# Small constants fetched behind the third step, a shorter lead for small transfers, and a shorter row of steps at the last tile's end, in a planned hybrid-decoder kernel

## The chip, the cores and the metric

The kernel runs on one core of one Trainium2 chip. The metric is the device time of one launch in microseconds (us), the median of several runs. Engines are named as the profile names them: PE (TensorE matmuls), DVE (VectorE), ACT (ScalarE), POOL (GpSimd) and SP (SyncE), which issues every DMA of this kernel.

## The reference

One layer of a hybrid decoder over a prompt of 2048 tokens and 8 single sample tokens, all in float32. The in-projection has 1024 rows and 4104 columns: eight groups of 512 columns, and 8 gate columns.

```python
h = rmsnorm(x, norm_w)
p = einsum('btd,de->bte', h, w_in)
hq, hf, hi, hz, gq, gk, gv, gz, gb, ga = split(p)
fg = lb + (1 - lb) * sigmoid(hf)               # lb from hg_lb_logits
o_hg, s_hg = hgrn2(hq, 1 - fg, hi, log(fg))    # 4 heads: S = diag(f) S + k v^T
qkv = silu(causal_conv4([gq | gk | gv], conv_w))
o_gdn, s_gdn = gated_delta(l2norm(q), l2norm(k), v, sigmoid(gb), g(ga))   # 4 heads
o = [rmsnorm(o_hg) * silu(hz) | rmsnorm(o_gdn) * silu(gz)]
y = rmsnorm(x + o @ w_out, final_norm)
```

The prompt runs through chunked forms of both recurrences; the samples take one recurrent step from given states. Outputs are both `y`, and the new states of prompt and samples.

## The kernel before, in words

**Arithmetic.** A float32 product is made of three PE passes over rounded parts: `xh`·`wh`, `xl`·`wh`, `xh`·`wl`, where the high part comes from a rounding copy and the low part is what that copy lost. For a piece of the in-projection's weights, DMA brings `raw` (256 KB), ACT writes `wh` and POOL writes `wl`. For tokens, PE transposes `xt` into `ps_x`, ACT writes `xh` and DVE `xl`. The out-projection has the same shape with `wor`, `woh`, `wol`, `oh` and `ol`.

**Order of the work.** `build` walks over a list of steps (loop at L1528): two halves of the prompt, four heads in each, and for each head the eight column groups, 512 tokens at a time. A step starts generators (projection, what follows it, the chains of the two recurrences); they record instructions through a wrapper, so that all instructions outside of PE bear line L404. Nothing is issued in the order of the program: `Model.plan` (L114) plays the recorded instructions forward and back on a model of the five queues (`play`, L155), eight passes, and fixes the best order found on every engine. For SP's DMAs it knows three things: the earliest moment of an issue, which is `AHEAD` = 30 us ahead of the instruction's due time (L173, L229); at most `LANES` = 8 transfers under way (L221); and one wire with a price by size and by the length of the contiguous run (L384).

**Constants.** Six small loads bring the convolution weights, the bound logits, the two head norms (all four into one tile `rows`, L1386 to L1390) and two gate vectors (`ald`). `small_ones` (L1402) then transposes `rows` on PE (`ps_rows`) and works out the constants that the heads' steps read; its last result is an integer `low`, which SP reads into a register.

**A gated-delta head.** For each head in each half of the prompt (eight times in all), a matrix is solved by blocks: DVE works `ti` out in 62 small steps (`xa`, `tm`, `ti`), four DMAs store it (`td<-ti`), four bring it back in another layout (`ut<-td`), DVE transposes it (`tn`), and PE goes on with `ps_v` and `ps_u`. The eight samples have a chain of their own beside it: `bcs<-dl` (4 KB, out), `db<-bcs` (the same spread over 128 partitions, 512 KB), eight scalings of `db` on ACT, `gate_s` and `a_bc` for the decay, and eight updates `S<-S,a_bc,db` on DVE.

**The end.** `out_proj` multiplies token tiles of 128 by `w_out`, adds the residual by halves of 512 columns (`xt<-ps_y,xt` on DVE), takes the sum of squares of each half on ACT (`jk`, `fss`), and `finish` (L1631) makes the reciprocal root on POOL (`frs`), scales by it and by `final_norm`, and stores. The last tile is scaled and stored in two halves.

## Time and profile before

| | us |
|---|---|
| median of 3 runs | 1253.29 |
| lowest, highest | 1249.16, 1253.98 |
| the profiled execution | 1249.11 |
| its span, first to last instruction | 1247.3 |
| PE busy | 1209.9 |
| DVE, ACT, POOL busy | 901.7, 516.8, 302.8 |

The profiled execution took 1249.11 us, of which 1247.3 are its span and 1.8 lie around it. It is as fast as the fastest of the three runs and 4.18 below their median. The mean granted clock of TensorE was 0.992 of full speed.

### The profile page before, as it was taken

To read this page: it belongs to the slowest core of one execution; us is meant where nothing else is said; L and a number is where in the kernel's file an instruction comes from. 1 tells how busy PE (TensorE), PEld (TensorE's weight loads), DVE (VectorE), ACT (ScalarE), POOL (GpSimd) and SP (SyncE) were. 2 spreads that over 40 slices of the span, in tenths; PEclk is the share of its full clock that TensorE was granted. 3 is DMA by queue.
4 is the path that set the end of the run, shared out by engine and by line. 5 is a ranking of instruction groups with operands and counts; after the bars stand their busy time and mean duration, and the time that the engine had idled before them with its cause. 6 is when DMAs were issued, how large, how long until landed. Compare 5 with 4: busy or idle time off the path is not lost.

```text
span 1247.3 us, 21811 instructions
## 1 busy us (share of the span) xinstructions
PE 1209.9 (97%) x8003; PEld 1045.9 (84%) x8003; DVE 901.7 (72%) x2301; ACT 516.8 (41%) x1517; POOL 302.8 (24%) x292
## 2 busy tenths in 40 slices
PE   7999999999899999989999999999999999999996
PEld 6988998989798889987787888887888887877885
DVE  5467986879687887889687868795787687854433
ACT  5436423633374326552464226323622464223221
POOL 5222221322133323312233214321322130000000
PEclk8999999999999999999999999999999999999998
DMA  6122443232433421333233332222233227442452
GB/s 198 40 59 60 63 60 87 63 73 57 128 86 73 105 74 35 106 120 77 59 93 70 41 77 47 58 52 61 68 71 77 56 68 222 150 130 88 142 161 91
DMA packets 143541, 107.51 MB, mean 86 GB/s; under 512 B 25611, under 2 KB 126281, under 8 KB 143417
## 3 DMA queue, kind: packets, MB, share of 16 engines
q1 hardware_dynamic: 143424, 106.02, 33.2%
q8 instruction: 65, 1.06, 0.3%
q14 instruction: 52, 0.42, 0.1%
HBM read 82.23 MB, written 23.91 MB: 85 GB/s over the span
## 4 chain that ended last, share of the span: by engine, by line
PE 81%; DMA 8%; DVE 6%; ACT 1%; SPq 1%; issue 1%; POOL 1%; POOLq 0%; DVEq 0%; ACTq 0%
PE ps_pj L517 47%; PE ps_y L517 14%; PE po_g L517 2%; PE po_h L517 2%; PE ps_kq L517 2%; PE ps_u L517 2%; DMA xt<-in_x_prompt_dram 1%; SPq L404 1%; DMA wor<-in_w_out_dram 1%; PE ps_s L517 1%; PE ps_g L517 1%; DMA raw<-in_w_in_dram 1%; PE ps_hu L517 1%; PE ps_ks L517 1%; PE ps_o L524 1%
## 5 line engine op out<-in xcount | busy, mean ns | idle before, releaser
L517 PE MATMUL ps_pj<-xh,wh 128*128 128x512 f32 (+2 forms) x1328 | 468.6, 353 | 7.4 <-ACT pre L404 2.9
L517 PE MATMUL ps_pj<-xl,wh 128*128 128x512 f32 (+2 forms) x1328 | 464.7, 350 | 0.4 <-DVE xl L404 0.4
L517 PE MATMUL ps_pj<-xh,wl 128*128 128x512 f32 (+2 forms) x1328 | 463.9, 350 | 0.7 <-POOL wl L404 0.6
L517 PEld LDWEIGHTS ps_pj<-xh,wh 128*128 128x128 f32 x1328 | 252.3, 190 | 33.3 <-ACT pre L404 3.3
L517 PEld LDWEIGHTS ps_pj<-xh,wl 128*128 128x128 f32 x1328 | 251.8, 190 | 26.0 <-POOL wl L404 1.1
L517 PEld LDWEIGHTS ps_pj<-xl,wh 128*128 128x128 f32 x1328 | 252.2, 190 | 24.4 <-DVE xl L404 0.6
L404 POOL TENSOR_TENSOR wl<-raw,wh 128x512 fp32r<-128x512 f32 x128 | 170.0, 1331 | 368.9 <-ACT wh L404 302.2
L404 ACT ACTIVATE wh<-raw 128x512 fp32r<-128x512 f32 x128 | 80.4, 630 | 162.5 <-PE ps_pj L517 115.8
L517 PE MATMUL ps_y<-woh,oh 128*128 128x512 f32 x256 | 101.0, 396 | 2.1 <-ACT woh L404 2.1
L517 PE MATMUL ps_y<-wol,oh 128*128 128x512 f32 x256 | 100.7, 394 | 0.3 <-DVE wol L404 0.3
L517 PE MATMUL ps_y<-woh,ol 128*128 128x512 f32 x256 | 100.2, 394 | 0.0
L404 DVE TENSOR_TENSOR tm<-xa,ti 128x248 f32<-128x248 f32 (+30 forms) x248 | 85.3, 344 | 16.9 <-DMA xa<-ad 9.0
L404 DVE TENSOR_TENSOR ti<-ti,tm 128x248 f32<-128x248 f32 (+30 forms) x248 | 90.7, 366 | 7.5
L404 ACT ACTIVATE jk<-xt 128x512 bf16<-128x512 f32 (+2 forms) x54 | 39.9, 740 | 117.3 <-DVE xt L404 79.1
L404 POOL TENSOR_TENSOR rso<-sso,mhalf 128x4 f32<-128x4 f32 x32 | 34.8, 1087 | 154.5 <-DVE sso L404 140.1
L517 PEld LDWEIGHTS ps_y<-woh,oh 128*128 128x128 f32 x256 | 48.1, 188 | 11.9 <-ACT woh L404 2.5
L517 PEld LDWEIGHTS ps_y<-wol,oh 128*128 128x128 f32 x256 | 48.2, 188 | 10.2 <-DVE wol L404 0.8
L517 PEld LDWEIGHTS ps_y<-woh,ol 128*128 128x128 f32 x256 | 48.1, 188 | 9.9 <-DVE ol L404 0.5
L404 POOL TENSOR_TENSOR frs<-fss,mhalf 128x1 f32<-128x1 f32 (+1 forms) x17 | 9.4, 555 | 191.5 <-DVE fss L404 191.5
L404 DVE TENSOR_TENSOR xt<-ps_y,xt 128x512 f32<-128x512 f32 (+1 forms) x34 | 23.5, 690 | 44.5 <-PE ps_y L517 44.2
L404 ACT ACTIVATE s_hg<-s_hg,e 128x128 f32<-128x128 f32 x80 | 31.8, 398 | 46.3 <-DVE s_hg L404 41.7
L404 ACT ACTIVATE uu<-ps_u,gam 128x128 f32<-128x128 f32 x64 | 23.4, 365 | 59.7 <-PE ps_u L517 59.3
(291 smaller groups left out, 2124.3 us busy)
## 6 DMA issues: line engine op xcount, KB each, us to landing
raw<-in_w_in_dram SPq DMA_DIRECT2D x128, 256.0 KB
xt<-in_x_prompt_dram SPq DMA_DIRECT2D x30, 512.0 KB
og_d<-sz SPq DMA_DIRECT2D x32, 256.0 KB
og<-og_d SPq DMA_DIRECT2D x32, 256.0 KB
out_dram<-xt SPq DMA_DIRECT2D x15, 512.0 KB
gb<-gate_r SPq DMA_DIRECT2D x16, 256.0 KB
xa<-ad SPq DMA_DIRECT2D x32, 128.0 KB
out_dram<-S SPq DMA_DIRECT2D x8, 512.0 KB
```

The costliest lines, as they stand in the source:

```text
L404: r = fn(*args, **kw)
L517: r = T.matmul(out, lhsT=lhsT, rhs=rhs, start=start, stop=stop)
L524: r = T.transpose(out, in_, idn)
```

## The change

Three things are done. The six small loads move into `small_ones`, and that generator starts at the fourth step (`i == 3`) and not ahead of the loop. In the planner, a transfer whose price on the wire is at most 0.5 us may be issued 15 us ahead of its due time and no more, others 30 as before, and in the first 16 us a transfer of short runs (under 2048 bytes) is priced 1.7 times as high. At the last tile, the first half's sum of squares gets its division and its epsilon early, and the first half its factor `final_norm`; at the end the second half is multiplied by `final_norm` on DVE, one instruction joins the two sums, and after the root ACT scales the first half and DVE the second.

```diff
-                    ready[i] = max(0.0, rank[i] - AHEAD)
+                    ready[i] = max(0.0, rank[i] - self.ahead(i))
...
             if k == "S":
+                if t < 16.0 and sort:
+                    late *= 1.7
                 wire = max(t + 0.8, wire)
...
-                    ready[j] = max(ready[j], rank[j] - AHEAD)
+                    ready[j] = max(ready[j], rank[j] - self.ahead(j))
...
+    def ahead(self, i):
+
+        return AHEAD if self.recs[i][2][1] > 0.5 else AHEAD / 2
...
-            return 0.4, size * 4e-3 / (330.0 if r >= 2048 else 130.0 if r >= 512 else 60.0 if r >= 128 else 6.5), False
+            return 0.4, size * 4e-3 / (330.0 if r >= 2048 else 130.0 if r >= 512 else 60.0 if r >= 128 else 6.5), r < 2048
...
-        rows = tmp.tile([64, P], F32, tag="tmp", name="rows")
-        Q.dma_start(rows[0:48], conv_w[0].rearrange("j (c p) -> (j c) p", p=P))
-        Q.dma_start(rows[48:56], hg_lb_logits.rearrange("l (c p) -> (l c) p", p=P))
-        Q.dma_start(rows[56:57], hg_out_norm)
-        Q.dma_start(rows[57:58], gdn_out_norm)
         wait(lambda: {0, 1} <= xs[0][2])
...
         def small_ones():
+            rows = tmp.tile([64, P], F32, tag="tmp", name="rows")
+            Q.dma_start(rows[0:48], conv_w[0].rearrange("j (c p) -> (j c) p", p=P))
+            Q.dma_start(rows[48:56], hg_lb_logits.rearrange("l (c p) -> (l c) p", p=P))
+            Q.dma_start(rows[56:57], hg_out_norm)
+            Q.dma_start(rows[57:58], gdn_out_norm)
+            Q.dma_start(ald[:, 0:4], gdn_a_log[0].partition_broadcast(P))
+            Q.dma_start(ald[:, 4:8], gdn_dt_bias[0].partition_broadcast(P))
             yield from ready(rows[0:58], slot=MID)
...
-        Q.dma_start(ald[:, 0:4], gdn_a_log[0].partition_broadcast(P))
-        Q.dma_start(ald[:, 4:8], gdn_dt_bias[0].partition_broadcast(P))
         consts = small_ones()
-        start(consts)
...
+            if i == 3:
+                start(consts)
             if i == 6:
...
                 def finish(y, n, ss, dst, pieces):
-                    V.tensor_tensor(ss[:n, 0:1], ss[:n, 0:1], ss[:n, 1:2], op=ALU.add)
-                    V.tensor_scalar(ss[:n, 0:1], ss[:n, 0:1], 1.0 / D, EPS, op0=ALU.mult, op1=ALU.add)
+                    if pieces > 1:
+                        V.tensor_tensor(y[:n, 512:], y[:n, 512:], fnb[:n, 512:], op=ALU.mult)
+                        V.scalar_tensor_tensor(ss[:n, 0:1], in0=ss[:n, 1:2], scalar=1.0 / D, in1=ss[:n, 0:1], op0=ALU.mult, op1=ALU.add)
+                    else:
+                        V.tensor_tensor(ss[:n, 0:1], ss[:n, 0:1], ss[:n, 1:2], op=ALU.add)
+                        V.tensor_scalar(ss[:n, 0:1], ss[:n, 0:1], 1.0 / D, EPS, op0=ALU.mult, op1=ALU.add)
...
+                    if pieces > 1:
+                        A.activation(y[:n, 0:512], y[:n, 0:512], AF.Copy, scale=rs[:n])
+                        V.tensor_scalar(y[:n, 512:], y[:n, 512:], rs[:n], None, op0=ALU.mult)
+                        Q.dma_start(dst[:, 512:], y[:n, 512:])
+                        Q.dma_start(dst[:, 0:512], y[:n, 0:512])
...
+                        if hf == 0 and i + 1 == len(order):
+                            V.tensor_scalar(ss[:n, 0:1], ss[:n, 0:1], 1.0 / D, EPS, op0=ALU.mult, op1=ALU.add)
+                            V.tensor_tensor(y[:n, 0:512], y[:n, 0:512], fnb[:n, 0:512], op=ALU.mult)
```

What the planner makes of it shows in the order of the queues. The first place is SP at the start of the program. Before (`rows` are the constants, `raw` the weights, `xt` the tokens, `csr` a convolution state):

```order
L404 DMA xt<-in_x_prompt_dram 128x512 x3
L404 DMA rows<-in_conv_w_dram 48x128
L404 DMA rows<-in_gdn_out_norm_dram 1x128
L404 DMA rows<-in_hg_lb_logits_dram 8x128
L404 DMA rows<-in_hg_out_norm_dram 1x128
L404 DMA xt<-in_x_prompt_dram 128x512
L404 DMA xt<-in_x_prompt_dram 128x1024
L404 DMA raw<-in_w_in_dram 128x4x128
```

With the change, the same queue from the fourth piece of `raw` on:

```order
L410 DMA raw<-in_w_in_dram 128x4x128
L410 DMA xt<-in_x_sample_dram 8x512
L410 DMA xt<-in_x_prompt_dram 128x1024
L410 DMA xt<-in_x_sample_dram 8x512
L410 DMA raw<-in_w_in_dram 128x4x128 x2
L410 DMA rows<-in_conv_w_dram 48x128
L410 DMA rows<-in_hg_lb_logits_dram 8x128
L410 DMA rows<-in_hg_out_norm_dram 1x128
L410 DMA rows<-in_gdn_out_norm_dram 1x128
L410 DMA csr<-in_state_gdn_conv_dram 24x512 x3
```

The constants stood ahead of the third piece of the weights; they now stand behind the sixth, and `ps_rows` has moved on PE behind 78 projecting matmuls and 44 transposes, where it had none and 16 ahead of it.

The second place is SP at the second half of the second solve, some 300 us into the run. Before:

```order
L404 DMA out_dram<-S 128x8x128
L404 DMA bcs<-dl 8x128
L404 DMA db<-bcs 128x1024
L404 DMA gate_s<-a_s 8x4
L404 DMA a_bc<-gate_s 128x32
L404 DMA td<-ti 32x256 x4
L404 DMA gb<-gate_r 128x512
L404 DMA raw<-in_w_in_dram 128x4x128
L404 DMA og_d<-sz 128x512
L404 DMA ut<-td 32x8x32 x4
L404 DMA gb<-gate_r 128x512
```

With the change:

```order
L410 DMA out_dram<-S 128x8x128
L410 DMA gb<-gate_r 128x512
L410 DMA td<-ti 32x256 x4
L410 DMA ut<-td 32x8x32 x4
L410 DMA og_d<-sz 128x512
L410 DMA gb<-gate_r 128x512
L410 DMA raw<-in_w_in_dram 128x4x128
L410 DMA bcs<-dl 8x128
L410 DMA og_d<-sz 128x512
L410 DMA db<-bcs 128x1024
L410 DMA gate_s<-a_s 8x4
L410 DMA raw<-in_w_in_dram 128x4x128
```

The two trips of the solve (`td`, `ut`) stood behind the samples' four transfers; now they stand ahead of them, and `a_bc` follows behind the last row shown.

The third place is DVE at the program's end: the additions of the last tile's two halves, and what follows. Before:

```order
L404 TENSOR_TENSOR xt_19868<-ps_y,xt_19868 128x512 x2
L404 TENSOR_TENSOR fss<-fss 128x1
L404 TENSOR_SCALAR fss<-fss 128x1
L404 SCALAR_TENSOR_TENSOR xt_19868<-xt_19868,frs,nwb 128x512 x2
L1820 UNCONDITIONAL_BRANCH x2
```

With the change:

```order
L410 TENSOR_TENSOR xt_19870<-ps_y,xt_19870 128x512
L410 TENSOR_SCALAR fss<-fss 128x1
L410 TENSOR_TENSOR xt_19870<-xt_19870,nwb 128x512
L410 TENSOR_TENSOR xt_19870<-ps_y,xt_19870 128x512
L410 TENSOR_TENSOR xt_19870<-xt_19870,nwb 128x512
L410 SCALAR_TENSOR_TENSOR fss<-fss 128x1
L410 TENSOR_SCALAR xt_19870<-xt_19870,frs 128x512
```

The second multiplication by `nwb` (which holds `final_norm`) stands ahead of the instruction that joins the two sums.

## Rows read from the trace of the kernel before

**Rows 1.** The page: busy time of the engines.
```profile
PE 1209.9 (97%) x8003; PEld 1045.9 (84%) x8003; DVE 901.7 (72%) x2301; ACT 516.8 (41%) x1517; POOL 302.8 (24%) x292
```

**Rows 2.** Waits of PE over the whole span: us in total, times, longest.
```profile
PE ps_rows L524 <- DMA rows<-in_conv_w_dram: 4.8, 1, 4.8
PE ps_v L517 <- DVE tn L404: 3.9, 2, 3.3
```

**Rows 3.** Timeline of SP, opening: start us, us, instruction, count.
```profile
6.91 2.68 SPq L404 DMA_DIRECT2D rows<-in_conv_w_dram  x1
...
13.58 0.22 SPq L404 DMA_DIRECT2D rows<-in_hg_out_norm_dram  x1
...
25.80 3.43 SPq L404 DMA_DIRECT2D raw<-in_w_in_dram  x2
```

**Rows 4.** Timeline of PE, opening; in brackets idle time and its releaser.
```profile
17.00 0.33 PE L524 MATMUL ps_rows<-ident,rows 58*128 58x58 f32 x1 [4.82 <-DMA rows<-in_conv_w_dram]
...
28.87 0.39 PE L517 MATMUL ps_pj<-xh,wl 128*128 128x256 f32 x1 [0.59 <-POOL wl L404]
```

**Rows 5.** The chain that ended last, opening: start us, us, what.
```profile
17.23 9.58 DMA raw<-in_w_in_dram
```

**Rows 6.** Two stretches by engine: busy us, instructions; PEclk; DMA share, GB/s.
```profile
30.00:40.00 10.00, 10.00 (x88) 9.87 (x86) 9.03 (x16) 6.66 (x18) 3.04 (x3) 1.00 0.17 44
...
325.00:330.00 5.00, 4.04 (x51) 3.58 (x54) 3.51 (x15) 0.00 (x0) 0.00 (x0) 0.66 0.19 44
```

**Rows 7.** Timeline of SP, 300 to 322 us.
```profile
301.40 1.90 SPq L404 DMA_DIRECT2D bcs<-dl  x1
311.54 0.34 SPq L404 DMA_DIRECT2D db<-bcs  x1
...
314.76 0.33 SPq L404 DMA_DIRECT2D a_bc<-gate_s  x1
315.14 1.82 SPq L404 DMA_DIRECT2D td<-ti  x4
...
317.52 0.40 SPq L404 DMA_DIRECT2D raw<-in_w_in_dram  x1
...
318.64 2.00 SPq L404 DMA_DIRECT2D ut<-td  x4
...
321.44 0.34 SPq L404 DMA_DIRECT2D og_d<-sz  x1
```

**Rows 8.** Timeline of DVE, 311 to 334 us.
```profile
311.52 0.17 DVE L404 TENSOR_TENSOR ti<-ti,tm 128x8 f32<-128x8 f32 x1
...
325.19 0.71 DVE L404 STREAM_TRANSPOSE tn<-ut 128x512 f32<-128x512 f32 x1 [3.63 <-DMA ut<-td]
...
333.35 0.86 DVE L404 COPY v<-ps_v 64x256 f32<-64x256 f32 x2
```

**Rows 9.** Timeline of ACT, first scaling of the samples' `db`.
```profile
315.23 0.40 ACT L404 ACTIVATE db<-db,smp 128x128 f32<-128x128 f32 x1 [5.20 <-DMA db<-bcs]
```

**Rows 10.** Timeline of SP and DVE, the first head's trip of the solve.
```profile
178.11 1.72 SPq L404 DMA_DIRECT2D td<-ti  x4
...
184.62 0.71 DVE L404 STREAM_TRANSPOSE tn<-ut 128x512 f32<-128x512 f32 x1 [0.60 <-DMA ut<-td]
```

**Rows 11.** Timeline of PE and DVE where the out-projection begins, and the last solve.
```profile
1050.36 0.72 PE L517 MATMUL ps_y<-woh,oh 128*128 128x512 f32 x2 [2.11 <-ACT woh L404]
...
1092.13 0.71 DVE L404 STREAM_TRANSPOSE tn<-ut 128x512 f32<-128x512 f32 x1
...
1113.39 0.69 PE L517 MATMUL ps_v<-tn,la 128*64 128x64 f32 x16
```

**Rows 12.** Timeline of DVE, the program's end.
```profile
1237.46 0.69 DVE L404 TENSOR_TENSOR xt<-ps_y,xt 128x512 f32<-128x512 f32 x1 [4.75 <-PE ps_y L517]
...
1238.94 0.16 DVE L404 TENSOR_TENSOR fss<-fss 128x1 f32<-128x1 f32 x1 [0.79 <-ACT jk L404]
...
1240.01 1.41 DVE L404 SCALAR_TENSOR_TENSOR xt<-xt,frs,nwb 128x512 f32<-128x512 f32 x2 [0.73 <-POOL frs L404]
```

More of the change, by code (lines that the diff above doesn't have):

```diff
@@ L1636, in finish @@
                     yield
+                    if pieces > 1:
[3 more added lines that the diff above has]
+                        Q.dma_start(dst[:, 0:512], y[:n, 0:512])
+                        alive[0] -= 1
+                        return
                     w = D // pieces
```

## Prediction

> **What bounds the kernel now.** I read the page first. PE is busy for 1209.9 of 1247.3 us, 97% [rows 1], and no other engine for more than 72%. So only 37 us are open to a change of order: stretches in which PE stands, and the stretches at half clock that follow some of them. The second view is PE's own waits, to see what they are made of: the longest is 4.8 us for `rows` at the opening, the next 3.3 us for `tn`, a step of the second head's solve [rows 2]. The third is the clock by stretch: from 325 to 330 us the granted clock is 0.66, that is 3.4 us at the lower of the two levels (1.2 GHz) and the rest at 2.4 GHz, which loses 1.7 us of work; from 330 on it is 1.00, with 88 matmuls in 10 us, 0.114 each [rows 6]. PE had stood for those 3.3 us, up to the end of `tn` at 325.90 [rows 8], just before it fell, so from 322.6 on. Last come the queues around the places that the change moves. All sums are made against the profiled execution, 1249.1 us.
>
> **The opening: -0.4 us.** The wait for `rows` looks like 4.8 us to be won: PE stands until 17.00 for constants [rows 4] whose first load is issued at 6.91 and whose last at 13.58, and which are there 3.2 us after that last issue [rows 3, 4]. But the opening doesn't end with it. PE waits again at 28.87 for `wl` [rows 4], which comes from the fourth piece of weights, under way from 17.23 to 26.81 [rows 5]. The loads of `rows` hold few bytes, and the big transfers ahead of that fourth piece are the same in both orders, so I expect it, and with it `wl`, at the same moment. What is won is what PE has done by then: in the new order six projecting matmuls and four transposes more stand ahead of this point, 10 x 0.114 = 1.1 us [rows 6]. Against that, the constants are now issued behind the sixth piece. That one is issued by 29.23 [rows 3]; four issues at some 0.3 us each, as short as the last one before was, bring 30.6, and 3.2 us of landing 33.8. PE comes to `ps_rows` earlier: of the instructions ahead of it some 37 are left after 28.87, which is 33.1. So 0.7 us of waiting is given back, and -0.4 is left. The bounds: nothing given back, -1.1; or the four loads take as long to issue as before (6.91 to 13.80, 6.9 us), then they land at 39.3, PE stands for 6.2 us, and the term is +5.1.
>
> The Trainium skill ("SBUF — State Buffer", section "The DMA setup-cost knee") gives every transfer a fixed cost of about 2 us. By it the constants would land at 32.6, ahead of PE, and the term would be -1.1. The row shows 3.2 us in a queue as full as this one, and I keep to the row.
>
> The same generator ends in the register that SP reads, and four pieces of weights stand behind that read; it is later by about as much as `ps_rows` is, and I cost it at nothing as long as `rows` isn't very late.
>
> **The second head's solve: -4.0 us.** This is the largest term. Before, `ti` is ready at 311.69 [rows 8], but `td` is issued at 315.14, because SP stands in `db<-bcs` (issued at 311.54, 10.1 us after `bcs<-dl`) and then waits for `a_bc` at 314.76 [rows 7]. `ut` follows at 318.64 behind three big transfers, and `tn` starts at 325.19 [rows 7, 8]. In the new order `td` and `ut` stand ahead of the samples' four transfers with nothing but one `gb` before them. An unhindered trip is shown by the first head: 178.11 to 184.62, 6.5 us [rows 10]. So `tn` can start at 311.7 + 6.5 = 318.2, and PE wants it at 322.6. The 3.3 us of standing go, and the 1.7 us of half clock with them: -5.0.
>
> What is late next is the samples' chain. `bcs` now stands behind a `raw` that was issued at 317.52, `db` behind a store of a gate that was issued at 321.44 [rows 7], and `a_bc` behind one more `raw`. `db` landed 3.7 us after its issue [rows 7, 9], so it is there at 325.5 and ACT can scale it; `a_bc` needs 3.2 us after `db`'s issue [rows 7], so it is issued at about 325 and lands behind 256 KB of weights, at 327 to 328. On DVE the first update `S<-S,a_bc,db` stands right behind the copies of `v`, which were at 333.35 [rows 8] and come at some 328.4 to 329.2 if 5 us are won. DVE is in order: if that update waits, the masks and the second level of the solve wait behind it, and PE for them. The margin is 1 to 2 us, and ACT must interleave seven scalings with the state steps as well. I take off 1.0 us for what gets through: -4.0. Bounds: -5.0, and +2.5 if the update waits for long (the first rival).
>
> **The out-projection's start: -1.0 us.** PE stands 2.11 us at 1050.36 for `woh` [rows 11]. In the new order three transfers of 384 KB in all (`xa`, for the last solve) stand behind the four pieces of `w_out` instead of ahead of them. Nothing shows whether these pieces wait for bytes or for a free buffer, so I take half. Bounds 0 and -2.1. What the later `xa` costs is covered: the last solve's `tn` runs at 1092.13 and PE first reads it at 1113.39 [rows 11], 21 us of slack for some 5 us of delay.
>
> **The end: 0.** Before, from the sums at 1238.94 to the scaling at 1240.01 pass 1.07 us, and the second half is scaled by 1240.01 + 1.41 = 1241.42, then stored [rows 12]. After, the multiplication by `nwb` stands ahead of the joining of the sums on DVE, and it can't start before ACT has read the half that it overwrites, so its 0.7 us (the addition of this size takes 0.69 [rows 12]) lie on the path. One small instruction falls away, 0.2. The root is then there at 1240.01 + 0.7 - 0.2 = 1240.5; scaling one half on each of two engines takes at most 0.7, and the second store goes out at 1241.3 to 1241.5, as before. The steps are fewer but the path is no shorter. Bounds -0.3 and +0.3. The early steps of the first half lie beside PE's last 11 us of matmuls.
>
> Everywhere else the order of SP's queue is nearly the same, and I cost it at nothing: PE's other waits (for `pre`, `szs`, `v`) stay. Every queue is redrawn, though, and a wait of 1 to 3 us may go or come anywhere.
>
> **The sum.** -0.4 - 4.0 - 1.0 + 0 = -5.4 us against 1249.1: 1243.7. The profiled execution is 4.2 below the median, so against the median of 1253.3 the forecast is **1247.9 us**, -0.43%. About 0.5% (6.3 us) is what a measurement of this kernel can tell from no change; -5.4 lies just inside.
>
> **The rivals.** *The samples' chain takes the place of the solve's wait.* If `bcs` again takes 10.1 us from its issue at 317.5 to `db`'s, `db` is issued at 327.6, `a_bc` at 330.8, and it lands at about 335. DVE then stands from 329.2 to 335, 5.8 us, and PE behind it, with the 1.7 us of half clock again: +2.5 in place of -4.0, a sum of +1.1, **1254.4 us**. For it: everything on SP is in order, and DVE places the update ahead of solver steps. Against it: the 10.1 us arose behind a store of 512 KB of short runs, which is long done by then.
>
> *Slower: PE stands at `ps_rows`, later and for longer.* The place is the opening. If the four loads wait for free lanes as they did before, the term is +5.1, and the clock falls after a wait of this length (as at 326 us), +1.7: together +6.8 in place of -0.4, a sum of +1.8, **1255.1 us**. If the register read then also holds SP's next four weights, some 5 us more come on top, 1260. It decides at 33.1 us: constants there by then cost nothing. Against it: the loads are issued where the queue thins (DMA share 0.17 from 30 to 40 us [rows 6]).
>
> *More goes than summed.* All of 5.0 at the solve, 2.1 at the out-projection, 1.1 at the opening and 1 to 2 us among the other waits: -9.7, **1243.6 us**.
>
> *It doesn't do what it says.* The planner only draws other waits of the same size: **1253 us**.
>
> **Chances.** The forecast's case 0.50 (1244.5 to 1250.5; 0.22 of it beyond the bound, since it lies just beside it); more than summed 0.18, all faster; the samples' chain 0.12 (0.02 slower); the late constants 0.11 (0.05 slower); only redrawn 0.09 (0.02 slower). That makes 0.40 faster, 0.51 the same, 0.09 slower. The range of 8 in 10 is 1240.5 to 1256.0: it takes in the case of more, both rivals' prices and an unchanged time, and leaves out their tails.
>
> **What would show it.** In the changed kernel's profile: `ps_rows` waiting less than 2 us at about 33, and the weights' wait near 28.9 still there; `tn` of the second solve at 318 to 321 and no wait of PE for it, and a clock of 1.00 from 325 to 330; DVE's first `S<-S,a_bc,db` there waiting less than 2 us; `woh` waited for by about 1 us; and from PE's last matmul to the end 10 us as before. I am wrong if PE's standing time in total isn't some 4 us smaller, if the largest wait is again in the second head, or if a new wait of over 3 us stands in a place that I costed at nothing.

## The result, and the profile after

The changed kernel takes **1238.54 us**, the median of five runs (1237.26 to 1240.10); the kernel before took 1253.29 in the same comparison (five runs, 1248.85 to 1253.98). The ratio is 0.9897, with a 95% interval of 0.9874 to 0.9920: faster by 1.0%, and 2.0 us below the range that was given. The profiled execution took 1238.38 us, its span is 1236.5, its mean granted clock 0.993 (before: 1249.11, 1247.3, 0.992). So the two profiled executions differ by 10.8 us of span, where the sum said 5.4.

The page of the changed kernel, busy time of the engines (answers to [rows 1]), then its waits of PE over the whole span (us in total, times, longest; answers to [rows 2]):

```profile
PE 1207.7 (98%) x8003; PEld 1045.1 (85%) x8003; DVE 908.5 (73%) x2302; ACT 516.7 (42%) x1518; POOL 310.2 (25%) x292
```

```profile
PE ps_x L530 <- DVE xt L410: 2.5, 1, 2.5
PE ps_x L530 <- DVE ss L410: 2.5, 1, 2.5
PE ps_pj L523 <- ACT vc L410: 2.4, 1, 2.4
...
PE ps_pj L523 <- ACT newc L410: 1.5, 1, 1.5
PE ps_v L523 <- DVE ut L410: 1.4, 1, 1.4
```

The 4.8 us for `rows` are gone, and so are the 3.3 for `tn`. Adding up all idle time of PE from its first matmul on, it stands for 17.9 us in place of 25.9. After 40 us one wait of over 1.5 us is left (2.4); before there were five, of 11.7 us together. A second view finds where the time came from: PE's busy time by stretch, at equal times. Changed kernel, then before (us, busy and count of PE, PEld, DVE, ACT, POOL; granted clock; DMA share, GB/s):

```profile
325.00:330.00 5.00, 3.32 (x30) 2.23 (x29) 4.04 (x9) 3.23 (x10) 1.27 (x1) 1.00 0.15 35
...
420.00:590.00 170.00, 161.44 (x1278) 145.66 (x1277) 139.00 (x350) 74.53 (x211) 46.28 (x42) 0.99 0.30 85
590.00:860.00 270.00, 268.87 (x1669) 224.51 (x1669) 208.80 (x550) 113.79 (x344) 80.04 (x65) 1.00 0.31 65
...
1030.00:1090.00 60.00, 59.57 (x263) 48.44 (x262) 46.80 (x117) 18.90 (x40) 3.81 (x5) 1.00 0.55 171
```

```profile
420.00:590.00 170.00, 164.23 (x1305) 148.89 (x1305) 139.14 (x357) 76.32 (x212) 45.10 (x43) 0.99 0.32 90
590.00:860.00 270.00, 264.74 (x1634) 219.96 (x1633) 208.66 (x556) 110.03 (x329) 73.98 (x63) 1.00 0.31 65
...
1030.00:1090.00 60.00, 57.51 (x255) 46.33 (x254) 47.89 (x115) 21.12 (x43) 2.28 (x4) 1.00 0.60 182
```

PE loses 2.8 us more than before from 420 to 590, and gains 4.1 from 590 to 860 and 2.1 at the out-projection. Set at equal numbers of finished matmuls (without `po_w`, 60 small matmuls at the start whose result nobody reads), the changed kernel is ahead by 1.0 us once a sixtieth of them is done (34.7 against 35.7), by 3.3 at 311 us, 6.2 at 416, 2.7 at 656, 5.5 at 844, 8.2 at 1026, 10.6 at 1088, and 10.2 at PE's last one (1227.2 against 1237.4). The rest, 0.6, lies behind PE's end (9.3 us there, 9.9 before; 9.1 to 10.1 over all profiles below, with the new end and without).

**The second head's solve.** SP, DVE and PE of the changed kernel (start us, us, instruction; in brackets idle time and what ended it), to be set beside [rows 7, 8]:

```profile
310.08 1.71 SPq L410 DMA_DIRECT2D td<-ti  x4
313.00 1.80 SPq L410 DMA_DIRECT2D ut<-td  x4
...
316.31 0.41 SPq L410 DMA_DIRECT2D bcs<-dl  x1
...
321.12 0.32 SPq L410 DMA_DIRECT2D db<-bcs  x1
...
324.07 0.32 SPq L410 DMA_DIRECT2D a_bc<-gate_s  x1
```

```profile
315.92 0.71 DVE L410 STREAM_TRANSPOSE tn<-ut 128x512 f32<-128x512 f32 x1 [0.64 <-DMA ut<-td]
...
321.61 0.42 DVE L410 TENSOR_SCALAR tn<-ps_u 32x256 f32<-32x256 f32 x1 [0.91 <-PE ps_u L523]
...
326.93 0.35 DVE L410 SCALAR_TENSOR_TENSOR S<-S,a_bc,db 128x128 f32<-128x128 f32 x1 [0.88 <-DMA a_bc<-gate_s]
```

```profile
326.15 0.69 PE L523 MATMUL ps_u<-ut,v 128*64 128x64 f32 x16 [0.34 <-PE po_h L523]
328.26 0.49 PE L523 MATMUL ps_ks<-s_gd,k 128*128 128x128 f32 x2 [0.77 <-DVE s_hg L410]
330.24 0.46 PE L523 MATMUL ps_hu<-vn,ktn 128*128 128x128 f32 x2 [0.81 <-DVE ut L410]
```

`td` and `ut` go out as planned, `tn` is made at 315.92 instead of 325.19, and the clock stays at 1.00 from 325 to 335. The samples' chain is late next, as expected: DVE stands 0.88 us for `a_bc`, and PE stands 1.9 us in three small waits. On DVE the first update `S` now stands behind the solver's next step, `tn<-ps_u`; in the kernel before it stands ahead of it:

```profile
328.86 1.66 DVE L404 SCALAR_TENSOR_TENSOR S<-S,a_bc,db 128x128 f32<-128x128 f32 x6
...
330.67 0.42 DVE L404 TENSOR_SCALAR tn<-ps_u 32x256 f32<-32x256 f32 x1
```

### The profile page after: what moved, and what is told of

It is laid out like the page before. It is cut to its first block, busy times and chain, and to the rows that moved or that the text cites. A ratio compares the mean times of both kernels' runs of the same rounds, so it can differ in the third digit from the quotient of the medians.

```text
span 1236.5 us, 21811 instructions
## 1 busy us (share of the span) xinstructions
PE 1207.7 (98%) x8003; PEld 1045.1 (85%) x8003; DVE 908.5 (73%) x2302; ACT 516.7 (42%) x1518; POOL 310.2 (25%) x292
## 4 chain that ended last, share of the span: by engine, by line
PE 86%; DMA 5%; DVE 4%; issue 1%; ACT 1%; SPq 1%; POOL 1%; POOLq 0%; ACTq 0%; DVEq 0%
PE ps_pj L523 52%; PE ps_y L523 14%; PE po_g L523 2%; PE po_h L523 2%; DMA xt<-in_x_prompt_dram 2%; PE ps_u L523 2%; PE ps_kq L523 2%; PE ps_s L523 1%; PE ps_ks L523 1%; PE ps_o L530 1%; PE ps_g L523 1%; PE ps_hu L523 1%; SPq L410 1%; PE ps_x L530 1%; PE ps_sc L523 1%
## 5 line engine op out<-in xcount | busy, mean ns | idle before, releaser
L523 PEld LDWEIGHTS ps_pj<-xl,wh 128*128 128x128 f32 x1328 | 251.4, 189 | 24.4 <-DVE xl L410 0.6
L410 POOL TENSOR_TENSOR wl<-raw,wh 128x512 fp32r<-128x512 f32 x128 | 174.6, 1366 | 344.4 <-ACT wh L410 331.6
L410 DVE TENSOR_TENSOR tm<-xa,ti 128x248 f32<-128x248 f32 (+30 forms) x248 | 87.1, 351 | 15.7 <-DMA xa<-ad 10.6
L410 POOL TENSOR_TENSOR frs<-fss,mhalf 128x1 f32<-128x1 f32 (+1 forms) x17 | 10.8, 632 | 185.8 <-DVE fss L410 169.0
L410 DVE SCALAR_TENSOR_TENSOR s_gd<-s_gd,el,ps_s 128x128 f32<-128x128 f32 x64 | 22.2, 346 | 37.9 <-PE ps_s L523 37.3
```

The lines of the kernel that those rows point to most:

```text
L410: r = fn(*args, **kw)
L523: r = T.matmul(out, lhsT=lhsT, rhs=rhs, start=start, stop=stop)
```

## The experiments

Two kinds of edit were tried. In the first, the program is edited and its planner draws all queues anew. In the second, the planner's result for the kernel before is written into the program as a table, and only named rows of that table are moved; then nothing else changes its place. (In the table V stands for DVE, A for ACT, G for POOL, T for PE and S for SP.) All ratios are to the kernel before in the same comparison (its medians there: 1252.7 to 1254.2). Each median is of four executions (e2, e4, e16, e17), five (before and the change, in the first comparison), six (e3) or nine to twelve; the last three columns come from the one that was profiled. "Standing" is all idle time of PE from its first matmul on, "half clock" PE's time at the lower level, up to its last matmul (twice the stretch's length by one minus its granted clock), "long" the number of PE's waits over 1.5 us after 40 us and their sum.

| run | us, median (runs from, to) | ratio, 95% interval | standing | half clock | long |
|---|---|---|---|---|---|
| before | 1253.29 (1248.9-1254.0) | | 25.9 | 13.7 | 5, 11.7 |
| changed | 1238.54 (1237.3-1240.1) | 0.990 [0.987, 0.992] | 17.9 | 10.2 | 1, 2.4 |
| e1 | 1252.38 (1249.9-1260.3) | 1.000 [0.998, 1.002] | 29.6 | 20.5 | 5, 12.3 |
| e2 | 1238.67 (1235.8-1241.3) | 0.987 [0.984, 0.991] | 21.6 | 10.2 | 0 |
| e3 | 1244.25 (1242.9-1247.3) | 0.993 [0.990, 0.996] | 23.3 | 10.2 | 2, 4.6 |
| e4 | 1236.08 (1235.4-1237.8) | 0.986 [0.983, 0.990] | 18.6 | 3.4 | 1, 1.7 |
| e5 | 1253.04 (1250.0-1257.5) | 1.000 [0.998, 1.002] | 27.0 | 20.5 | 5, 11.8 |
| e6 | 1249.60 (1242.9-1252.8) | 0.996 [0.993, 0.998] | 27.2 | 17.1 | 4, 9.1 |
| e7 | 1254.04 (1247.8-1259.2) | 0.999 [0.996, 1.001] | 32.6 | 23.9 | 7, 18.7 |
| e8 | 1249.54 (1247.0-1256.7) | 0.997 [0.994, 0.999] | 24.8 | 13.7 | 4, 8.9 |
| e9 | 1250.47 (1247.4-1255.7) | 0.998 [0.997, 1.000] | 25.7 | 20.5 | 3, 10.0 |
| e10 | 1254.04 (1251.7-1260.3) | 1.001 [0.999, 1.004] | 32.0 | 27.3 | 3, 15.3 |
| e11 | 1253.75 (1251.2-1255.4) | 1.001 [0.999, 1.003] | 28.7 | 20.5 | 5, 13.3 |
| e12 | 1252.42 (1251.2-1256.6) | 1.000 [0.999, 1.001] | 30.0 | 17.1 | 4, 10.8 |
| e13 | 1248.07 (1245.2-1252.2) | 0.997 [0.994, 1.000] | 24.4 | 13.7 | 2, 5.6 |
| e14 | 1255.76 (1253.1-1259.5) | 1.003 [1.001, 1.005] | 28.2 | 23.9 | 3, 7.1 |
| e15 | 1243.80 (1239.7-1245.8) | 0.994 [0.991, 0.996] | 21.3 | 6.8 | 2, 3.8 |
| e16 | **1230.07** (1229.7-1231.1) | 0.983 [0.978, 0.988] | 13.0 | 3.4 | 0 |
| e17 | 1233.63 (1231.8-1236.8) | 0.985 [0.981, 0.987] | 17.1 | 3.4 | 2, 4.9 |
| e18 | 1246.63 (1241.6-1249.2) | 0.994 [0.992, 0.996] | 23.2 | 17.1 | 4, 9.3 |

In all twenty profiles PE's end less its standing time less half of the half-clock time lies between 1202.5 and 1206.9 us. So the profiles of this family, whose PE ends lie from 1219 to 1249 us, differ in these two columns and, beyond them, by no more than 4.4 us.

### The kernel before, again, and each edit alone

e1 is the kernel before, unedited. 

> The kernel before, unchanged, run again. Its five runs so far lie at 1249 (two) and at 1253.5 (three), with nothing between; the forecast was made on the profiled execution (1249.1) and then carried to the median by +4.2. Theory A: the 4.4 us between the two groups are one stall with its half clock that only some executions take (the changed kernel's runs, 1237.3 to 1240.1, have no such gap); then new runs fall at 1249 and 1253.5 again, and an execution of the slower kind shows a mean clock lower by about 0.002 and one wait of PE more. Rival B: the gap is chance of five runs; then the new ones fill the space between.

Its twelve executions lie from 1249.85 to 1260.31, and with the 19 of the same kernel beside them they don't fall into two groups; those were a chance of five runs. Of the other half of the theory the lower clock holds (0.990 in e1's profile, 0.992 in before's); one wait of PE more doesn't, there are five long ones in both. The page and three stretches of e1's profile, same instructions and same order as before:

```profile
PE 1214.3 (97%) x8003; PEld 1048.4 (84%) x8003; DVE 901.7 (72%) x2301; ACT 516.5 (41%) x1517; POOL 303.1 (24%) x292
```

```profile
325.00:330.00 5.00, 1.69 (x15) 1.21 (x16) 1.44 (x7) 0.63 (x1) 1.26 (x1) 0.79 0.64 175
330.00:335.00 5.00, 5.00 (x91) 4.60 (x90) 3.32 (x11) 0.63 (x1) 0.15 (x1) 0.52 0.04 11
...
1055.00:1065.00 10.00, 7.29 (x24) 5.41 (x25) 8.49 (x19) 4.08 (x7) 0.00 (x0) 0.83 0.45 140
```

PE is busy for 4.4 us more than in [rows 1] with the same 8003 matmuls, largely because more of them ran at half clock (20.5 us in place of 13.7, which costs 3.4): at the 3.3 us wait it is 6.9 us (granted clock 0.79, then 0.52) in place of the 3.4 of [rows 6], and a stretch behind the wait for `woh` near 1058 has come in, where before's profile had none. So in these two profiles the five long waits are the same, and the half clock that comes with them isn't. It shows over the 130 executions of this kernel in the comparisons below, too: the mean time of the ten with a granted clock of 0.986 or 0.987 is 1258.4 us, that of the 23 with 0.992 is 1251.1.

e2, e3 and e4 take one part of the change each:

```diff
 e2: the lines of finish and of the last tile alone
 e3: rows and ald moved into small_ones, start(consts) at i == 3, alone
 e4: the lead alone
-                    ready[i] = max(0.0, rank[i] - AHEAD)
+                    ready[i] = max(0.0, rank[i] - self.ahead(i))
...
```

e2: 

> The kernel before with only the last tile's shorter end. Theory A (the end is worth what its own place shows): from PE's last matmul to the end of the span 9.3 us instead of 9.9, and no place before the last tile is meant to move. Rival B (any edit makes the planner draw all queues anew): the order of DVE differs in hundreds of places, PE's waits before the last tile change by several us in sum, of either sign, and the time moves by much more than 0.6 us, up or down.

e3: 

> The kernel before with only the six constant loads moved behind the fourth step. Theory A: the opening alone gains, about 1 us by the time PE has done a sixtieth of its matmuls (35.7 before, 34.7 with the change), PE does not stand for the constants at 17 us, and the second head's solve at 326 us stands as before (3.3 us and 1.7 us at half clock). Rival B: the gain at the solve comes from the redrawn order and not from the lead of small transfers; then it can go here too.

e4: 

> The kernel before with only the shorter lead of small transfers (15 us instead of 30). Theory A: this is the part that moves the samples' transfers behind the solve's; the second solve's tn then starts near 316 to 319 us, PE's wait for it and the stretch at half clock go, -2.5 to -5 us there; the opening still stands 4.8 us for the constants. Rival B: the solve keeps its wait here, and it took the other parts to move it.

e2 gives 14.6 us, e3 9.0 (3.4 of them at the opening: a sixtieth of the matmuls is done at 32.3), e4 17.2: together 41, where the change with all three gives 14.8. In e2 and e3 the 3.3 us wait at the solve is gone too, though neither has the shorter lead. Parts that add up to nearly three times the whole were not tested alone: each is another draw of all queues. That called for tables.

### Pieces tested with the order held

```diff
+PLAN = {'V': [...], 'A': [...], 'G': [...], 'T': [...], 'S': [...]}
-        order = best[1]
+        order = PLAN
 e5: and the new end; no other row moved
 e6: S (SP) at the second solve; on V the eight updates S behind the second copies of v;
     on A the eight scalings of db behind the next wh
-outS bcs db gate_s a_bc td td td td gb raw og_d ut ut ut ut gb og_d raw
+outS gb td td td td ut ut ut ut og_d gb raw bcs og_d db gate_s raw a_bc
 e7: S as in e6, a_bc one place earlier; the scalings on A in one row;
     V as before: the updates S ahead of tn<-ps_u
```

e5: 

> The last tile's shorter end on the order of the kernel before, written out as a table, so that nothing else moves. The end alone gave 1238.7 when the planner was let run. Theory A (redrawing): here the time stays near that of before, lower by 0.6 us at its place (9.3 us from PE's last matmul to the end instead of 9.8), so within 1249 to 1260 with a median near 1252.5, and PE's waits are those of before (3.3 at 326, 2.1 near 675, 2 near 852 and 1050). Rival B (the end itself is worth 14 us by some way not seen): about 1239.

No difference, to within 3 us: the end by itself is worth nothing that shows, so e2's 14.6 us were its redraw.

e6: 

> The order of the kernel before, written out as a table, with one piece changed: at the second head's solve td and ut go ahead of the samples' four transfers on SP, their eight scalings on ACT go behind the next wh, and the eight updates S on DVE go behind the second copies of v. All the rest is as before. Theory A: tn starts near 316 to 318 us, PE's 3.3 us of standing and the half clock behind it go, some 1 to 2 us of new small waits come: -2.5 to -5 us in the profile, a median near 1249. Rival B (the place is worth nothing, PE stands a little later for the same time): the median stays at 1252 to 1253.

4.6 us by the medians (1254.20 to 1249.60; the interval allows 2.6 to 8.8). The 3.3 us wait is gone, 1.6 us in two small ones are left. e6's waits of PE from 300 to 345 us, and the first update on DVE:

```profile
PE ps_hu L520 <- DVE ut L407: 1.2, 1, 1.2
PE ps_ks L520 <- DVE s_hg L407: 0.4, 1, 0.4
```

```profile
330.73 0.35 DVE L407 SCALAR_TENSOR_TENSOR S<-S,a_bc,db 128x128 f32<-128x128 f32 x1 [0.69 <-DMA a_bc<-gate_s]
```

e7: 

> As the run before it, but DVE's eight updates S stay where they stood, ahead of the solve's next steps; and a_bc goes one place forward on SP, the eight scalings stand together on ACT. Theory of the first rival of the forecast: DVE now stands for a_bc and db until 327 to 328 us ahead of tn<-ps_u, so PE waits 3 to 6 us there and falls to half clock: the gain at this place is gone, 1252 to 1256. Rival: the samples' transfers are there by then and the gain is the same as with the updates moved.

The same move on SP, without that on DVE, gives nothing that shows. e7's waits of PE from 300 to 345 us, DVE, and SP's issue of `a_bc`:

```profile
PE ps_v L520 <- DVE ut L407: 5.2, 1, 5.2
```

```profile
329.47 1.66 DVE L407 SCALAR_TENSOR_TENSOR S<-S,a_bc,db 128x128 f32<-128x128 f32 x6 [4.85 <-ACT db L407]
331.15 0.42 DVE L407 TENSOR_SCALAR tn<-ps_u 32x256 f32<-32x256 f32 x1
```

```profile
326.55 0.32 SPq L407 DMA_DIRECT2D a_bc<-gate_s  x1
```

Here the samples' updates stand ahead of the solver's `tn`, wait 4.85 us, and PE stands 5.2 us behind them. The view names the scalings of `db`; but the trace has `a_bc` landing at the same moment, 329.35, 2.8 us after its issue, and the two can't be told apart. This is the first rival, made by hand.

### Neutral redraws

e8 moves the planner's lead by a thirtieth, e14 likewise; e11 and e15 move the new factor of the change by a seventeenth; e12 takes the two planner lines other than the lead alone.

```diff
 e8, e14 (before)
-AHEAD = 30.0
+AHEAD = 29.0          e14: 31.0
 e11, e15 (changed)
-                    late *= 1.7
+                    late *= 1.6          e15: 1.8
```

e8: 

> The kernel before with one number of the planner changed that is no part of the change: the lead of all transfers 29 us instead of 30. The planner draws all queues anew. Theory A (the order of before is an unlucky draw, and any other draw is better by 9 to 17 us, as the three parts alone were): 1236 to 1246. Rival B (draws scatter on both sides of before, and the three parts are better for reasons of their own): as likely above 1253 as below; a single value above 1250 speaks for it.

e14: 

> A second draw of the kernel before: the lead 31 us instead of 30. Theory D (the change has no gain of its own; draws of the planner before and of the planner after come from one spread, 1236 to 1254): anywhere in it. Rival E (the changed planner's draws are better on the whole): this one at 1249 to 1254, as the other two draws of the planner before with the same program.

e11: 

> The changed kernel with one number of its planner changed a little: 1.6 instead of 1.7 for the early price of short runs, which bears on the first 16 us alone. All queues are drawn anew. If the change itself gives its 15 us, 1237 to 1241 again; if it is a draw among draws, the time moves by several us, anywhere in 1234 to 1250, with the number of PE's waits of over 1.5 us.

e15: 

> A second neutral draw of the changed kernel: 1.8 instead of 1.7 for the early price of short runs. Theory D: anywhere in 1236 to 1254; a value above 1246 makes two of three draws that have no gain. Rival E: 1236 to 1243, and the draw with 1.6 was the unlucky one.

e12: 

> The kernel before with only the higher price of short runs in the first 16 us, the last part of the change by itself. Theory A (a draw): somewhere in 1234 to 1252, and its PE's end equals 1204 us plus PE's standing time plus half of the time at half clock, as in all ten profiles so far. Rival B (this part has an effect of its own): the opening alone differs from before, by -1 to +1 us, and the waits from 300 us on are those of before.

Edits that mean nothing moved before's time by -4.7 (e8, against 1254.20) and +2.8 us (e14, against 1252.96), and that of the change to 1253.75 and 1243.80. The whole gain is lost in e11. DVE there, and its waits of PE from 300 to 345 us:

```profile
328.68 1.93 DVE L410 SCALAR_TENSOR_TENSOR S<-S,a_bc,db 128x128 f32<-128x128 f32 x3 [1.94 <-DMA a_bc<-gate_s]
330.63 0.42 DVE L410 TENSOR_SCALAR tn<-ps_u 32x256 f32<-32x256 f32 x1
```

```profile
PE ps_v L523 <- DVE ut L410: 4.0, 1, 4.0
```

SP has the new order in e11 too (`td` at 312.68, `bcs` at 317.44); the rival decided itself on DVE. That is one wait of the five long ones that e11 has. e12 lands where before does, with a wait of 4.5 us for `tn`; e14 lies 1.8 us above the ranges that either theory gave it.

### Mending the other long waits by hand

e9 moves five pieces in before's table, one at each of PE's long waits, e10 four of them (all but the solve's), and e13 adds to e9 that seven steps of the last solve go behind the weights on DVE:

```diff
 e9: the solve as in e6; A at 532 and 675 us; V at 852 us; S at the out-projection:
-xa xa xa wor wor wor wor
+wor wor wor wor xa xa xa
 e13, on V as well:
-tm ti tm ti tm ti tm wol wol wol wol
+wol wol wol wol tm ti tm ti tm ti tm
```

e9: 

> The order of the kernel before as a table with five small pieces changed, one at each of PE's five long waits behind the opening: the second solve (as in the run of that alone, -4.6), a wh that stood ahead of thz, xh and t near 530 us on ACT, the first scaling of db ahead of pre and vv near 674 us on ACT, ek ahead of the solve's v near 850 us on DVE, and xa ahead of the last four pieces of w_out near 1040 us on SP. Theory A: what the changed kernel and the other draws gain is that few waits of over 1.5 us are left, each of which costs itself and, in most executions, 1.7 us for a stretch at half clock; before has five (11.7 us). With all five gone or halved: -3.3 -2 -2 -1.7 -2 and some 4 to 5 us of half clock, so 1238 to 1243. Rival B: the waits only move to the next place, or the gain lies in hundreds of small differences; then no better than the solve's alone, 1248 to 1250.

e10: 

> As the run before it, without the piece at the second solve. Theory A: the four others by themselves are worth -2 -2 -1.7 -2 and some 3 us of half clock: 1243 to 1247; with the solve's piece they add up to the run of all five. Rival B: 1252 to 1254, as before.

e13: 

> As the run of all five pieces, mended at the last one: there DVE had stood 6.5 us for the later xa, ahead of the wol that PE waited for (6.5 us at 1051); now the seven tm and ti steps that read xa stand behind the four wol on DVE as well. Theory A (PE's long waits and the half clock behind them are what the draws differ by): that wait goes to under 1 us, and with four of five places mended the median falls from 1250.5 to 1242 to 1246. Rival B (waits only move on, the whole is worth what the second solve is): 1248 to 1251 again.

None gets near the change, and each misses the range that theory A gave it. e9 differs from e10 by the solve's piece alone and is 3.6 us faster, a second reading of what that place gives. In e9, DVE and PE where the out-projection begins:

```profile
1047.69 0.42 DVE L407 TENSOR_TENSOR tm<-xa,ti 128x248 f32<-128x248 f32 x1 [6.50 <-DMA xa<-ad]
...
1050.66 2.73 DVE L407 SCALAR_TENSOR_TENSOR wol<-wor,nrm,woh 128x512 fp32r<-128x512 f32 x4
```

```profile
PE ps_y L520 <- DVE wol L407: 6.5, 1, 6.5
```

With `xa` behind the weights on SP and still ahead of them on DVE, DVE stands 6.5 us for `xa`, and PE for `wol` behind it. With DVE's rows moved too (e13), PE's wait there is still 3.9:

```profile
PE ps_y L520 <- DVE ol L407: 3.9, 1, 3.9
```

`ol` stands on DVE behind the steps that were moved (1047.36 to 1051.17). A wait that is mended in one place comes back at the next that was laid out around it. So two of the long waits were never mended here (1.7 us at 532 and these 3.9), and what all five are worth together isn't shown.

### With and without the shorter lead

e16 is the change without its end, e17 the lead alone with another value, e18 the change without the lead.

```diff
 e17, against e4
-        return AHEAD if self.recs[i][2][1] > 0.5 else AHEAD / 2
+        return AHEAD if self.recs[i][2][1] > 0.5 else 14.0
```

e16: 

> The changed kernel without the last tile's shorter end, the other two parts as they are. By place the end is worth 0 to 0.6 us, so if parts add up: 1238.5 to 1239.5. Theory D: a further draw, anywhere in 1236 to 1254.

e17: 

> A second draw of the shorter lead alone: 14 us for small transfers instead of 15. So far five draws with the shorter lead have medians of 1230.1, 1236.1, 1238.5, 1243.8 and 1253.8 (mean 1240.5), six without it 1238.7, 1244.3, 1249.5, 1252.4, 1253.3 and 1255.8 (mean 1249.0). Theory D (one spread for all draws): anywhere in 1230 to 1256, about 1245. Theory E (the shorter lead gives better draws on the whole, by some 8 us): 1232 to 1245.

e18: 

> The changed kernel without the shorter lead: constants moved, early price, shorter end. Theory D: anywhere in 1230 to 1256, about 1245. Theory E: 1244 to 1256, above the draw with the lead of 14 us. In either: a median of 1249 or more goes with PE standing over 2.5 us between 310 and 335 us, one of 1245 or less goes without, as in all eleven draws so far.

e16 is faster than both kernels, by 1.7% and by 0.7% (1230.07 to 1238.54). Its page, and its longest waits of PE (the second is the one ahead of the first matmul):

```profile
PE 1204.4 (98%) x8003; PEld 1040.6 (85%) x8003; DVE 902.4 (73%) x2301; ACT 514.1 (42%) x1517; POOL 303.8 (25%) x292
```

```profile
PE ps_x L530 <- DVE xt L410: 5.4, 6, 1.4
PE po_w L539 <- POOL ident masks.py:199: 1.6, 1, 1.6
PE ps_y L523 <- ACT woh L410: 1.1, 1, 1.1
```

No wait reaches 1.5 us once the opening is over, and its runs lie within 1.4 us. It lies 6 us under the lowest time that was expected of it. As the end is worth nothing (e5), what e16 has over the change is its draw.

Six draws have the shorter lead (the change, e4, e11, e15, e16, e17): 1230.1 to 1253.8, mean 1239.3. Seven planned ones have not (before, e2, e3, e8, e12, e14, e18): 1238.7 to 1255.8, mean 1248.7. The difference of 9.3 has a standard error of 4.1, worked out from the scatter of the two sets (8.4 and 5.9). So the shorter lead probably makes good draws likelier. It isn't settled: one draw scatters by as much as the whole effect. What the lead does in every draw of it is to put `td` and `ut` ahead of `bcs` and `db` on SP (e4: `td` at 307.79, `bcs` at 318.79), in the seven others they stand behind. That place is worth 4.6 us (e6; 3.6 between e10 and e9) if DVE's order goes along, and nothing that shows if it doesn't (e7; in e11 the wait came back).

The solve's place parts the thirteen draws better than the lead does. The five with a wait of PE over 2.5 us between 310 and 335 us have medians of 1249.5 to 1255.8 (before, e8, e11, e12, e14), the eight without 1230.1 to 1246.6; the means lie 14 us apart. e2, e3 and e18 are among the eight with `td` behind `bcs` and `db`. By hand the place gave 4.6, so most of the 14 goes along with it and isn't caused by it as far as is shown.

## Why the prediction was wrong

**The solve: right in mechanism, near in size.** -4.0 was forecast. From 311 to 416 us the changed kernel gains 2.9, and the same move with all else held gives 4.6 (e6). What gets through at the samples' chain is 1.9 us of small waits rather than 1.0. The first rival is a real one: it was made in e7 and came by itself in e11. The change escaped it with 0.88 us of wait on DVE, because its draw put the updates behind `tn<-ps_u`.

**The opening: right in sign.** -1.0 in place of -0.4. PE comes to `ps_rows` at 33.43 (33.1 by the forecast) and doesn't wait there. The two waits that now stand at the opening are new ones. PE of the changed kernel:

```profile
11.27 1.33 PE L530 MATMUL ps_x<-ident,xt 128*128 128x128 f32 x8 [2.54 <-DVE xt L410]
18.69 0.34 PE L530 MATMUL ps_x<-ident,xt 128*128 128x128 f32 x1 [2.48 <-DVE ss L410]
...
33.43 0.27 PE L530 MATMUL ps_rows<-ident,rows 58*128 58x58 f32 x1
```

So the 4.8 us became 5.0 in other places, and what is won is in part the weights' wait at 28.87 [rows 4], which is gone: the forecast took the fourth `wl` to come at the same moment in both orders, but POOL ends it at 28.05 in place of 28.82. (The forecast's sum for the constants is 0.2 us too long: 29.23 and four issues of 0.3 make 30.4, not 30.6.) The fourth load of `rows` is issued at 29.70 for 0.24 us; PE reads them 3.5 us after that end, so the rival with the late constants fell. The 2 us that the Trainium skill ("SBUF — State Buffer", section "The DMA setup-cost knee") gives a transfer and the 3.2 of the row both lie below these 3.5; no run here shows which is right.

**The out-projection's start: half of it missed.** -2.4 in place of -1.0: nothing of the wait for `woh` is left with the pieces of `w_out` ahead of `xa` on SP. PE of the changed kernel, beside [rows 11]:

```profile
1038.25 0.50 PE L523 MATMUL ps_y<-woh,oh 128*128 128x512 f32 x1 [0.38 <-ACT oh L410]
```

**The end: right, from a wrong place.** 0 was forecast, and e5 gives 0. But the third place of the order that is shown ahead of the prediction comes from the second of two copies of that loop in the program, which this input doesn't run. In the copy that runs, the joining of the sums stands ahead of the multiplication. DVE and POOL of the changed kernel, then POOL of before:

```profile
1228.78 0.16 DVE L410 SCALAR_TENSOR_TENSOR fss<-fss 128x1 f32<-128x1 f32 x1 [0.85 <-ACT jk L410]
1228.86 0.68 DVE L410 TENSOR_TENSOR xt<-xt,nwb 128x512 f32<-128x512 f32 x1
...
1229.98 0.49 DVE L410 TENSOR_SCALAR xt<-xt,frs 128x512 f32<-128x512 f32 x1 [0.44 <-POOL frs L410]
```

```profile
1229.09 0.86 POOL L410 TENSOR_TENSOR frs<-fss,mhalf 128x1 f32<-128x1 f32 x1 [10.14 <-DVE fss L410]
```

```profile
1239.43 0.55 POOL L404 TENSOR_TENSOR frs<-fss,mhalf 128x1 f32<-128x1 f32 x1 [10.27 <-DVE fss L404]
```

The 0.7 us aren't on the path: the multiplication runs beside the root. The path from the joining of the sums to the scaling is 1.20 us (1228.78 to 1229.98) in place of 1.07, though an instruction fell away, because POOL's root takes 0.86 beside that multiplication and took 0.55 alone.

**Where it failed.** The step is "Everywhere else the order of SP's queue is nearly the same, and I cost it at nothing". Lined up by names and shapes, 430 of SP's 500 transfers and 1655 of DVE's 2302 instructions keep their order; a change of one unrelated number leaves 446 and 1825 (e8). So the change redraws about as much as an edit that means nothing, and that is not costed by looking at SP. The stretches outside the four places gave 3.9 us net (the 10.8 of span less 1.0, 2.9, 2.4 and the 0.6 at the end), made of gains (waits of 0.96 at 274, 1.72 at 852 and half of one at 675 us gone) and of a loss from 420 to 590. The text said that a wait "may go or come anywhere", and gave it 1 to 3 us; the redraws show -8 to +15 us for the change (e16, e11) and -5 to +3 for the kernel before (e8, e14). The range was too narrow for that on its lower side: of the thirteen draws five lie under 1240.5, and none above 1256.0. There is luck in the size, too: the three draws of the change with its factor at 1.6, 1.7 and 1.8 have a mean of 1245.4, which is inside the range, and the one forecast here is 6.8 below it.

The second failing step is "against the median of 1253.3": the 4.2 us between before's profiled execution and its median were carried to the new kernel. The changed kernel's profiled execution is 0.2 below its median. The offset belongs to the one kernel: at before's long waits half clock comes in some executions and not in others (e1), its profiled execution had less of it than e1's, and the changed kernel has one such wait left. That this is all of the 4.2 isn't shown. These two steps, 3.9 and 4.0 us, and 1.5 us from the sizes of the four terms (-6.9 measured, -5.4 in the sum), make up the 9.4 between 1247.9 and 1238.5.

Of the signs that were named, those that would have shown it wrong stayed away: standing time fell by 8.0 us (4 were asked for), the second head no longer has the longest wait, and no new wait is over 3 us. Three others missed to the better side: the weights' wait near 28.9 is gone, `tn` comes at 315.9 and not at 318 to 321, and `woh` isn't waited for. They could not tell a larger gain from the one forecast; the rival "more goes than summed" was the nearest, and it counted 1 to 2 us among the other waits.

What stays open: why a draw with the shorter lead is better on the whole, and whether it is; and what beside the solve makes the change's draw good, since mending before's long waits by hand (e9, e10, e13) didn't reproduce it.

## What to carry to other kernels

Where a planner orders all queues, an edit's time is its mechanism and a redraw: time some neutral redraws first (here draws scatter by 6 to 8 us, half a per cent or more), and credit an edit only with what it gives when the rest of the order is held in a table. A move on one in-order queue can need a move on the queue behind it: the solve's two transfers were worth 4.6 us with DVE's updates moved, and nothing that shows without. PE's long waits are paid in standing and, in part of the executions, once more in half clock; but of those mended by hand only the solve's paid.

## What the runs showed of the hardware

One program in one order spreads by 15 us: the kernel before ran from 1245.7 to 1260.8 in 130 executions over all comparisons. Of the two draws without a long wait, four executions each, e16 spreads by 1.4 and e2 by 5.5, so the long waits alone don't set it. While PE worked, stretches at half clock (1.2 of 2.4 GHz) lasted 3.4 or 6.8 us in the profiles, and behind 40 us most of them came at a wait of PE of more than 1.5 us; at the same wait they came in one execution of the kernel before and not in another (e1 near 1058 us), and what decides that isn't shown.

POOL's last root, of 128 numbers, takes 0.55 us in the fourteen profiles where it runs alone, and 0.86 or 0.87 in the six (the change, e2, e5, e11, e15, e18) where a DVE multiplication that reads two operands runs beside it. The Trainium skill ("SBUF — State Buffer", section "Who interferes with whom") says that DVE's second pair of ports to this memory is GpSimd's only one, and that one engine holds it at a time; the traces agree, with 0.3 us.
